# Seven-product weight pairs of a hybrid decoder trunk: the rounded weights times both activation parts in one matmul, and a weight sum made by DMA inside SBUF

## The chip, the cores and the metric

The kernel runs on one core of a Trainium2 chip. The metric is the device time of one execution in microseconds (us), the median of several runs. The engines are named as the profile names them: PE (TensorE matmuls), PEld (its weight loads), DVE (VectorE), ACT (ScalarE), POOL (GpSimd), SP (SyncE, which here only issues transfers).

## The reference

Two residual layers on x of 512 positions by 2048 features, all in float32, and a final RMSNorm.

```python
def reference(...):
    h = x
    hn = rmsnorm(h, norm_w[0]); h = h + hybrid_layer(hn, ...)      # DeltaNet heads and dilated attention
    hn = rmsnorm(h, norm_w[1]); h = h + shortconv_layer(hn, ...)
    return rmsnorm(h, final_norm_w)

def shortconv_layer(h, w_in, conv_w, w_out):                       # w_in 2048 x 12288, w_out 3072 x 2048
    gate_b, gate_c, u, z = jnp.split(h @ w_in, 4, axis=-1)
    y = gate_b * causal_depthwise_conv(gate_c * u, conv_w)
    return (y * jax.nn.silu(z)) @ w_out
```

The change touches `h @ w_in` of the second layer alone.

## The kernel before, in words

Every weight matrix is read from HBM in blocks, split into a rounded part `w_hi` and a rest `w_lo` (ACT rounds, DVE subtracts), and each product of float32 numbers is made of three matmuls in a fast format: hi by x_hi, hi by x_lo, lo by x_hi. Layer one and the last projection do so with 512 columns (`mm3`, L149 to L154).

`h @ w_in` of layer two is 96 blocks of 128 outputs. They are computed two at a time by `pair` (L867), 48 times, each as a 2 by 2 block product with seven half-size products instead of eight: weights `wa` and `wb` (two output blocks) are halved along the features, the activation is halved along features and positions, and seven sums or differences of the activation quarters (`forms`, made once, L771) are kept as tiles `fm`, each 128 by 256 in a rounded and a rest part. One product (`product`, L856) walks j over 8 blocks of 128 features and issues three matmuls of 256 columns per j (L862 to L864). So there are 48 x 7 x 8 = 2688 steps j.

The seven products of a pair, here P1 to P7, go into three PSUM banks: P1 and P5 into `acc`, P2, P4 and P6 into `sb`, P3 and P7 into `sc`. Their weights are in this order q11, q11 + s1, s3, s1, q12, q12 + (q11 + s1), q22. The raw tiles q11, s1, s3, q12 and q22 hold 512 KB each: five SP transfers from HBM (L870, L872, L873, L875, L876), and on POOL two transfers that add from HBM into SBUF (L871 into s1, L874 into s3). The two other sums are DVE additions (L884 for q11 + s1, L903 for q12). Raw tiles come from eight buffers, two of pool `wp` and `NRAW` = 6 of pool `w4`.

`split_w` (L849) takes the next of three `w_hi` and three `w_lo` buffers. So the split for one product can start only when the product three places earlier has used its buffer up: the split for P1 waits for P5 of the pair before, that for P2 for P6.

PE runs its instructions in the written order. The other engines' order is set by a list scheduler at build time, with loads and splits raised in priority by `SPLIT_AHEAD`; on the chip each engine then takes its own list strictly in order. Results are taken out of PSUM 256 columns at a time (ACT copies at L882 and L901, DVE at L888, L896, L897, L906, L910).

Of the kernel before, what the change touches and what calls it, by code (L numbers as in the profile page):

```python
# [14 lines left out]
P = 128  # L15
T = 512
# [14 lines left out]
NMT2 = 4 * NCH  # L31
NX2 = 24
NJ1 = 3
NRAW = 6
SPLIT_AHEAD = 600


# [37 lines left out]
def hybrid_trunk(ctx: ExitStack, tc: tile.TileContext, xT, w1, w1o, w2, w2o, nw, dcw, scw, hp, dnw, cst, msk, rope,  # L75
                 out, dbg=None):
    nc = tc.nc
    V, A, G, PE, SP = nc.vector, nc.scalar, nc.gpsimd, nc.tensor, nc.sync
    flow = Flow()
# [9 lines left out]
    def bank(name="m"):  # L89
        return mp.tile([P, T], F32, name=name, tag="m")  # L90
# [77 lines left out]
    def new_acc():  # L168
        return acc_p.tile([P, T], F32, name="acc")
# [34 lines left out]
    first = []  # L204
    with tc.tile_pool(name="ini", bufs=3) as ini:
# [29 lines left out]
        first = accs  # L235
# [334 lines left out]
    with tc.tile_pool(name="dn", bufs=2, side="right") as dn:  # L570
# [135 lines left out]
        for g in range(QKH):  # L706
# [52 lines left out]
    H = T // 2  # L759
    NJ = KT // 2  # L760
    rd2 = []
    slots = iter([(x2p, "x2", NX2)] * NX2 + [(xp, "x", 32)] * 32)
    fm = [[None] * NJ for _ in range(7)]

    def form(i, j, src):
        pool, tag, bufs = next(slots)
        t = pool.tile([P, 2, H], F32R, name="fm", tag=tag, bufs=bufs)
        A.activation(t[:, 0, :], src, AF.Copy)
        V.tensor_tensor(t[:, 1, :], src, t[:, 0, :].bitcast(F32), op=ALU.subtract)  # L769
        fm[i][j] = (t[:, 0, :], t[:, 1, :])  # L770

    def forms(pool, j, he, ho):
        e1, e2, o1, o2 = he[:, 0:H], he[:, H:T], ho[:, 0:H], ho[:, H:T]
# [65 lines left out]
    with tc.tile_pool(name="w4", bufs=1) as w4, tc.tile_pool(name="sc", bufs=1, side="right") as sc:  # L839

        def raw():
            i = nraw[0]
            nraw[0] += 1
            pool, tag, bufs = ((wp, "w_raw", 2), (w4, "w_raw4", NRAW))[i % (2 + NRAW) >= 2]
            return pool.tile([P, NJ, P], F32, name="w_raw", tag=tag, bufs=bufs)

        nraw = [0]

        def split_w(src):  # L849
            hi = wp.tile([P, NJ, P], F32R, name="w_hi", tag="w_hi", bufs=3)  # L850
            A.activation(hi, src, AF.Copy)  # L851
            lo = wp.tile([P, NJ, P], F32R, name="w_lo", tag="w_lo", bufs=3)
            V.tensor_sub(lo, src, hi.bitcast(F32))  # L853
            return hi, lo

        def product(w, f, o, first):  # L856
            hi, lo = w
            o = o[:, 0:H]
            for j in range(NJ):
                flow.poll()  # L860
                xh, xl = fm[f][j]
                PE.matmul(o, hi[:, j, :], xh, start=first and j == 0, stop=False, skip_group_check=not first)  # L862
                PE.matmul(o, hi[:, j, :], xl, start=False, stop=False, skip_group_check=not first)  # L863
                PE.matmul(o, lo[:, j, :], xh, start=False, stop=j == NJ - 1, skip_group_check=not first)  # L864
                flow.t += 0.36

        def pair(wa, wb, c1, c2):  # L867
            with tc.high_priority(offset=SPLIT_AHEAD):
                q11, s1, s3, q12, q22 = (raw() for _ in range(5))
                SP.dma_start(s1, wb[:, 0:NJ, :])  # L870
                G.dma_start(s1, wb[:, NJ:KT, :], accum_op=ALU.add)  # L871
                SP.dma_start(q11, wa[:, 0:NJ, :])  # L872
                SP.dma_start(s3, wa[:, 0:NJ, :])  # L873
                G.dma_start(s3, wb[:, 0:NJ, :], accum_op=ALU.add)  # L874
                SP.dma_start(q12, wa[:, NJ:KT, :])  # L875
                SP.dma_start(q22, wb[:, NJ:KT, :])  # L876
            a, b, c = new_acc(), bank("sb"), bank("sc")
            with tc.high_priority(offset=SPLIT_AHEAD):
                w = split_w(q11)
            product(w, 0, a, True)  # L880
            a1 = sc.tile([P, H], F32, name="a1", bufs=2)
            A.activation(a1, a[:, 0:H], AF.Copy)  # L882
            with tc.high_priority(offset=SPLIT_AHEAD):
                V.tensor_tensor(q11, q11, s1, op=ALU.add)  # L884
                w = split_w(q11)
            product(w, 5, b, True)
            e = sc.tile([P, H], F32, name="e", bufs=2)
            V.tensor_tensor(e, b[:, 0:H], a1, op=ALU.add)  # L888
            with tc.high_priority(offset=SPLIT_AHEAD):
                w = split_w(s3)  # L890
            product(w, 6, c, True)
            with tc.high_priority(offset=SPLIT_AHEAD):
                w = split_w(s1)
            product(w, 4, b, False)
            b2 = sc.tile([P, H], F32, name="b2", bufs=1)
            V.tensor_tensor(b2, b[:, 0:H], a1, op=ALU.add)  # L896
            V.tensor_tensor(c2[:, H:T], c[:, 0:H], b2, op=ALU.subtract)  # L897
            with tc.high_priority(offset=SPLIT_AHEAD):
                w = split_w(q12)
            product(w, 1, a, False)  # L900
            A.activation(c1[:, 0:H], a[:, 0:H], AF.Copy)  # L901
            with tc.high_priority(offset=SPLIT_AHEAD):
                V.tensor_tensor(q12, q12, q11, op=ALU.add)  # L903
                w = split_w(q12)
            product(w, 2, b, False)
            V.tensor_tensor(c1[:, H:T], b[:, 0:H], a1, op=ALU.add)  # L906
            with tc.high_priority(offset=SPLIT_AHEAD):
                w = split_w(q22)
            product(w, 3, c, False)
            V.tensor_tensor(c2[:, 0:H], c[:, 0:H], e, op=ALU.subtract)  # L910

        def ctile(w=T):
            return sc.tile([P, w], F32, name="ct", tag="ct", bufs=6)

        rbc2 = sc.tile([P, T], F32, name="rbc2")
        for c in range(NCH):
            cc, cu = ctile(), ctile(T + 2)
            G.memset(cu[:, 0:2], 0.0)
            u = cu[:, 2:T + 2]
            pair(w2[4 * c], w2[4 * c + 1], cc, u)  # L920
            if c == 0:
                flow.drain()
# [12 lines left out]
            V.scalar_tensor_tensor(gz, gz, 1.0, cz, op0=ALU.add, op1=ALU.mult)
            V.tensor_tensor(gz, gz, cc, op=ALU.mult)
            yt = sc.tile([P, T], F32, name="y2", bufs=2)
            V.scalar_tensor_tensor(yt, cb, 0.5, gz, op0=ALU.mult, op1=ALU.mult)
            if c < NCH - 1:
                SP.dma_start(Y2d[c], yt)  # L940
        ys = [None] * NCH
        for c in range(NCH):
            if c < NCH - 1:
                yl = sc.tile([P, T], F32, name="yl", tag="ct", bufs=6)
                SP.dma_start(yl, Y2d[c])
            else:
                yl = yt
            ys[c] = split_y(PX if c < 16 else (x2p, "x2", NX2), yl)
# [129 lines left out]
```

## Time and profile before

| | us |
|---|---|
| median of 3 runs (2819.26 to 2821.29) | 2820.0 |
| the profiled execution: its own time | 2821.6 |
| the profiled execution: span of the trace | 2819.8 |
| PE busy in the span | 2774.8 |
| DVE, ACT, POOL busy | 1798.9, 1091.6, 160.6 |
| the 48 pairs, by the first and last start of L862 | 1549.7 to 2526.2 |

The span is one profiled execution. Matmuls overlap in a pipeline, so a matmul's own duration is longer than the distance from one start to the next; the distance is what the stage costs. PEclk is the granted clock of TensorE as a share of 2.4 GHz, so 0.50 is 1.2 GHz. "To landing" of a transfer counts from its issue to its last byte. A name in square brackets behind a row is what ended the engine's idle time before it.

### The profile page before, as it was taken

How to read it: one execution, taken by the hardware profiler on the slowest of the kernel's cores; microseconds unless marked ns; L12 is line 12 of the kernel's file. 1: busy time of each engine (PE TensorE's matmuls, PEld its weight loads, DVE VectorE, ACT ScalarE, POOL GpSimd, SP SyncE). 2: the span in 40 equal slices, each digit the busy share in tenths (PEclk: the TensorE clock that was granted, in tenths of full speed). 3: DMA queues.
4: the chain of work that ended last, by engine and by line, in shares of the span. 5: the costliest groups of instructions: out<-in, count | busy, mean ns of one | idle time of the engine just before them, and what ended most of it. 6: DMA issues, size and time to landing. Idle time of an engine off the chain costs nothing.

```text
span 2819.8 us, 41852 instructions
## 1 busy us (share of the span) xinstructions
PE 2774.8 (98%) x16648; PEld 2463.6 (87%) x16648; DVE 1798.9 (64%) x2707; ACT 1091.6 (39%) x1803; POOL 160.6 (6%) x226
## 2 busy tenths in 40 slices
PE   8999999999999999999999899999999999999998
PEld 6888888888887888888887899999999999997887
DVE  7766999555445655665334677777777777774223
ACT  5443444444432323234323444444444444443221
POOL 3110000000000000000000100000000000000000
PEclk9999999999999999999999999999999999999999
DMA  5655223322224333333444767776677676754333
GB/s 170 183 169 186 90 87 127 111 88 86 94 86 127 124 105 110 115 113 112 127 127 135 217 181 200 186 204 182 190 191 197 187 191 188 194 164 141 114 112 112
DMA packets 163059, 410.58 MB, mean 146 GB/s; under 512 B 41184, under 2 KB 55776, under 8 KB 162608
## 3 DMA queue, kind: packets, MB, share of 16 engines
q1 hardware_dynamic: 149040, 357.57, 39.4%
q0 software_dynamic: 13824, 50.34, 10.1%
q8 instruction: 131, 2.15, 0.3%
q14 instruction: 64, 0.52, 0.1%
HBM read 373.44 MB, written 34.41 MB: 145 GB/s over the span
## 4 chain that ended last, share of the span: by engine, by line
PE 93%; DVE 3%; DMA 2%; issue 1%; ACT 1%; SPq 0%; DVEq 0%; POOL 0%; ACTq 0%; POOLq 0%
PE acc L151 17%; PE acc L153 17%; PE acc L152 17%; PE sb L862 5%; PE sb L864 5%; PE sb L863 5%; PE sc L862 3%; PE sc L864 3%; PE acc L862 3%; PE acc L864 3%; PE sc L863 3%; PE acc L863 3%; PE p L96 2%; DMA w_raw<-in_w_dram 1%; DVE w_lo L146 1%
## 5 line engine op out<-in xcount | busy, mean ns | idle before, releaser
L151 PE MATMUL acc<-x_hi,w_hi 128*128 128x512 f32 x1536 | 622.5, 405 | 1.6 <-DVE cv_raw L319 1.6
L153 PE MATMUL acc<-x_hi,w_lo 128*128 128x512 f32 x1536 | 602.3, 392 | 5.1 <-DVE w_lo L146 5.1
L152 PE MATMUL acc<-x_lo,w_hi 128*128 128x512 f32 x1536 | 600.6, 391 | 0.5 <-DVE x_lo L200 0.3
L144 ACT ACTIVATE w_hi<-w_raw 128x1024 fp32r<-128x1024 f32 (+2 forms) x302 | 308.9, 1024 | 683.9 <-PE acc L152 513.9
L851 ACT ACTIVATE w_hi<-w_raw 128x1024 fp32r<-128x1024 f32 x336 | 356.3, 1061 | 559.2 <-PE acc L863 165.8
L146 DVE TENSOR_TENSOR w_lo<-w_raw,w_hi 128x1024 fp32r<-128x1024 f32 (+2 forms) x302 | 363.6, 1206 | 315.1 <-ACT w_hi L144 314.4
L853 DVE TENSOR_TENSOR w_lo<-w_raw,w_hi 128x1024 fp32r<-128x1024 f32 x336 | 411.0, 1224 | 160.9 <-ACT w_hi L851 159.0
L153 PEld LDWEIGHTS acc<-x_hi,w_lo 128*128 128x128 f32 x1536 | 289.2, 188 | 69.6 <-DVE w_lo L146 7.2
L151 PEld LDWEIGHTS acc<-x_hi,w_hi 128*128 128x128 f32 x1536 | 290.1, 189 | 57.4 <-DVE cv_raw L319 1.8
L152 PEld LDWEIGHTS acc<-x_lo,w_hi 128*128 128x128 f32 x1536 | 290.3, 189 | 55.8 <-DVE x_lo L200 1.8
L862 PE MATMUL sb<-fm,w_hi 128*128 128x256 f32 x1152 | 325.9, 283 | 0.0
L864 PE MATMUL sb<-fm,w_lo 128*128 128x256 f32 x1152 | 325.2, 282 | 0.0
L863 PE MATMUL sb<-fm,w_hi 128*128 128x256 f32 x1152 | 324.5, 282 | 0.0
L151 PE MATMUL acc<-y_hi,w_hi 128*128 128x512 f32 (+1 forms) x792 | 307.6, 388 | 4.8 <-ACT y_hi L732 3.2
L152 PE MATMUL acc<-y_lo,w_hi 128*128 128x512 f32 (+1 forms) x792 | 305.7, 386 | 3.5 <-DVE y_lo L734 3.5
L153 PE MATMUL acc<-y_hi,w_lo 128*128 128x512 f32 (+1 forms) x792 | 305.8, 386 | 1.2 <-DVE w_lo L146 1.2
L862 PE MATMUL sc<-fm,w_hi 128*128 128x256 f32 x768 | 218.0, 284 | 5.5 <-ACT w_hi L851 5.5
L862 PEld LDWEIGHTS sb<-fm,w_hi 128*128 128x128 f32 x1152 | 219.7, 191 | 0.0
L863 PEld LDWEIGHTS sb<-fm,w_hi 128*128 128x128 f32 x1152 | 218.9, 190 | 0.0
L864 PEld LDWEIGHTS sb<-fm,w_lo 128*128 128x128 f32 x1152 | 218.5, 190 | 0.0
L864 PE MATMUL sc<-fm,w_lo 128*128 128x256 f32 x768 | 217.5, 283 | 0.5 <-DVE w_lo L853 0.5
L863 PE MATMUL acc<-fm,w_hi 128*128 128x256 f32 x768 | 216.0, 281 | 1.3 <-DVE fm L769 1.3
(241 smaller groups left out, 4322.5 us busy)
## 6 DMA issues: line engine op xcount, KB each, us to landing
w_raw<-in_w_dram SPq DMA_DIRECT2D x428, 512.0 KB, 4.4
w_raw<-in_w_dram POOLq DMA_DIRECT2D x96, 512.0 KB, 7.1
w_raw<-in_w1o_dram SPq DMA_DIRECT2D x48, 512.0 KB, 3.6
w_raw<-in_w2o_dram SPq DMA_DIRECT2D x48, 512.0 KB, 3.6
Y2d<-y SPq DMA_DIRECT2D x23, 256.0 KB, 5.3
yl<-Y2d SPq DMA_DIRECT2D x23, 256.0 KB, 4.4
xr<-in_xT_dram SPq DMA_DIRECT2D x16, 256.0 KB, 4.3
KQd<-kq SPq DMA_DIRECT2D x8, 512.0 KB, 5.1
```

The lines of the kernel that those rows point to most:

```text
L96: PE.matmul(o, lhsT, rhs, start=start, stop=stop)
L144: A.activation(hi, raw, AF.Copy)
L146: V.tensor_sub(lo, raw, hi.bitcast(F32))
L151: PE.matmul(acc, hi, xh, start=first, stop=False)
L152: PE.matmul(acc, hi, xl, start=False, stop=False)
L153: PE.matmul(acc, lo, xh, start=False, stop=last)
L851: A.activation(hi, src, AF.Copy)
L853: V.tensor_sub(lo, src, hi.bitcast(F32))
L862: PE.matmul(o, hi[:, j, :], xh, start=first and j == 0, stop=False, skip_group_check=not first)
L863: PE.matmul(o, hi[:, j, :], xl, start=False, stop=False, skip_group_check=not first)
L864: PE.matmul(o, lo[:, j, :], xh, start=False, stop=j == NJ - 1, skip_group_check=not first)
```

## The change

In `product`, a step j issues two matmuls: the rounded weights times both parts of `fm` side by side (512 columns, L861), and the rest of the weights times the rounded part (256 columns, L863). The left half of the bank then holds hi by x_hi plus lo by x_hi, the right half hi by x_lo. Copies and sums out of PSUM become 512 wide, and a new DVE addition `folded` (L868) adds the two halves, twice per pair. PE's list shrinks from 15691 to 13003 rows, which is by 2688.

In `pair`, q11 is split for P1 as soon as it is there; s3 is begun by an ACT copy of q11 (L877) instead of a second transfer from HBM; and q11 + s1 is made by a third POOL transfer, which adds s1 to q11 from SBUF to SBUF (L879), instead of a DVE addition. `NRAW` is 5.

```diff
-NRAW = 6
+NRAW = 5
...
-                PE.matmul(o, hi[:, j, :], xh, start=first and j == 0, stop=False, skip_group_check=not first)
-                PE.matmul(o, hi[:, j, :], xl, start=False, stop=False, skip_group_check=not first)
-                PE.matmul(o, lo[:, j, :], xh, start=False, stop=j == NJ - 1, skip_group_check=not first)
-                flow.t += 0.36
+                fx = fm[f][j]
+                PE.matmul(o, hi[:, j, :], fx.rearrange("p a t -> p (a t)"), start=first and j == 0, stop=False,
+                          skip_group_check=not first)
+                PE.matmul(o[:, 0:H], lo[:, j, :], fx[:, 0, :], start=False, stop=j == NJ - 1,
+                          skip_group_check=not first)
+                flow.t += 0.346
+
+        def folded(dst, w):
+            V.tensor_tensor(dst.rearrange("p (a t) -> p a t", a=2), w[:, :, 0:H], w[:, :, H:T], op=ALU.add)
...
                 SP.dma_start(s1, wb[:, 0:NJ, :])
                 G.dma_start(s1, wb[:, NJ:KT, :], accum_op=ALU.add)
                 SP.dma_start(q11, wa[:, 0:NJ, :])
-                SP.dma_start(s3, wa[:, 0:NJ, :])
+                w0 = split_w(q11)
+                A.activation(s3, q11, AF.Copy)
                 G.dma_start(s3, wb[:, 0:NJ, :], accum_op=ALU.add)
+                G.dma_start(q11, s1, accum_op=ALU.add)
                 SP.dma_start(q12, wa[:, NJ:KT, :])
                 SP.dma_start(q22, wb[:, NJ:KT, :])
...
-                w = split_w(q11)
-            product(w, 0, a, True)
-            a1 = sc.tile([P, H], F32, name="a1", bufs=2)
-            A.activation(a1, a[:, 0:H], AF.Copy)
-            with tc.high_priority(offset=SPLIT_AHEAD):
-                V.tensor_tensor(q11, q11, s1, op=ALU.add)
                 w = split_w(q11)
             product(w, 5, b, True)
-            e = sc.tile([P, H], F32, name="e", bufs=2)
-            V.tensor_tensor(e, b[:, 0:H], a1, op=ALU.add)
+            e = sc.tile([P, T], F32, name="e", bufs=1)
+            V.tensor_tensor(e, b, a1, op=ALU.add)
...
-            V.tensor_tensor(c2[:, H:T], c[:, 0:H], b2, op=ALU.subtract)
+            w2t = sc.tile([P, 2, T], F32, name="ww", tag="ww", bufs=2)
+            V.tensor_tensor(w2t[:, 1, :], c, b2, op=ALU.subtract)
...
-            V.tensor_tensor(c1[:, H:T], b[:, 0:H], a1, op=ALU.add)
+            V.tensor_tensor(w1t[:, 1, :], b, a1, op=ALU.add)
+            folded(c1, w1t)
...
-            V.tensor_tensor(c2[:, 0:H], c[:, 0:H], e, op=ALU.subtract)
+            V.tensor_tensor(w2t[:, 0, :], c, e, op=ALU.subtract)
+            folded(c2, w2t)
```

Two places show how the lists move. On POOL, about the middle of the stage, before (w_raw_17268 and w_raw_17502 are the s1 tiles of two pairs that follow each other, w_raw_17269 and w_raw_17503 their s3 tiles):

```order
L871 DMA w_raw_17268<-in_w2_dram 128x1024
L874 DMA w_raw_17269<-in_w2_dram 128x1024
L871 DMA w_raw_17502<-in_w2_dram 128x1024
L874 DMA w_raw_17503<-in_w2_dram 128x1024
L918 MEMSET ct_17499 128x2
L871 DMA w_raw_17733<-in_w2_dram 128x1024
L874 DMA w_raw_17734<-in_w2_dram 128x1024
```

and after (w_raw_17362, 17544 and 17723 are q11 of three pairs that follow each other; one, two and so on higher are s1 and s3 of the same pair):

```order
L874 DMA w_raw_17545<-in_w2_dram 128x1024
L879 DMA w_raw_17362<-w_raw_17363 128x1024
L924 MEMSET cu_17542 128x2
L878 DMA w_raw_17546<-in_w2_dram 128x1024
L874 DMA w_raw_17724<-in_w2_dram 128x1024
L879 DMA w_raw_17544<-w_raw_17545 128x1024
L878 DMA w_raw_17725<-in_w2_dram 128x1024
```

Each pair has a third transfer, L879, and in the pairs shown the s1 transfer of the pair that follows stands just ahead of it; over the whole list that is so in 27 of 48 pairs.

On DVE, before, from the last split of a pair (w_raw_17271, its q22) to the third of the next (w_raw_17501 is its q11, 17502 its s1, 17503 its s3):

```order
L853 TENSOR_TENSOR w_lo_17463<-w_raw_17271,w_hi_17461 128x1024
L853 TENSOR_TENSOR w_lo_17518<-w_raw_17501,w_hi_17516 128x1024
L884 TENSOR_TENSOR w_raw_17501<-w_raw_17501,w_raw_17502 128x1024
L906 TENSOR_TENSOR ct_17265<-sb_17280,a1_17310 128x256
L932 TENSOR_TENSOR ct_17265<-ct_17265,rbc_84 128x512
L853 TENSOR_TENSOR w_lo_17549<-w_raw_17501,w_hi_17547 128x1024
L910 TENSOR_TENSOR ct_17266<-sc_17281,e_17341 128x256
L935 SCALAR_TENSOR_TENSOR gzs_17491<-gzs_17491,ct_17265 128x512
L853 TENSOR_TENSOR w_lo_17579<-w_raw_17503,w_hi_17577 128x1024
```

and after, the same place (w_raw_17366 is the q22 of the pair that ends, w_raw_17544 the q11 of the next):

```order
L853 TENSOR_TENSOR w_lo_17513<-w_raw_17366,w_hi_17511 128x1024
L853 TENSOR_TENSOR w_lo_17554<-w_raw_17544,w_hi_17552 128x1024
L910 TENSOR_TENSOR ww_17486<-sb_17380,a1_17398 128x512
L868 TENSOR_TENSOR ct_17360<-ww_17486 128x512
L938 TENSOR_TENSOR ct_17360<-ct_17360,rbc_84 128x512
L915 TENSOR_TENSOR ww_17464<-sc_17381,e_17420 128x512
L941 SCALAR_TENSOR_TENSOR gzs_17534<-gzs_17534,ct_17360 128x512
L868 TENSOR_TENSOR ct_17361<-ww_17464 128x512
L942 TENSOR_TENSOR gzs_17534<-gzs_17534,ct_17180 128x512
L944 SCALAR_TENSOR_TENSOR y2_17538<-ct_17361,gzs_17534 128x512
L853 TENSOR_TENSOR w_lo_17584<-w_raw_17544,w_hi_17582 128x1024
L853 TENSOR_TENSOR w_lo_17606<-w_raw_17546,w_hi_17604 128x1024
```

The addition L884 between the first and the second split of q11 is gone from DVE, and the second split now stands behind the output work of the pair that ends.

## Rows read from the trace of the kernel before

**Rows 1.** The page: busy time of each engine, share of the span, instructions.

```profile
PE 2774.8 (98%) x16648; PEld 2463.6 (87%) x16648; DVE 1798.9 (64%) x2707; ACT 1091.6 (39%) x1803; POOL 160.6 (6%) x226
```

**Rows 2.** Busy time by stretch, 200 us inside the stage; first row: columns.

```profile
core 0: us, PE busy (x) PEld busy (x) DVE busy (x) ACT busy (x) POOL busy (x), PEclk, DMA share, GB/s
...
1800.00:2000.00 200.00, 200.00 (x1679) 200.00 (x1678) 155.03 (x185) 85.40 (x101) 18.66 (x26) 1.00 0.72 191
```

**Rows 3.** Timeline of PE, 256-column matmuls (start us, us, engine, line, names).

```profile
1600.00 0.29 PE L864 MATMUL sb<-fm,w_lo 128*128 128x256 f32 x1
...
1603.95 0.28 PE L864 MATMUL sc<-fm,w_lo 128*128 128x256 f32 x1
```

**Rows 4.** Timeline of PE: 512-column matmuls, then a 512 followed by a 256.

```profile
1001.04 0.39 PE L151 MATMUL acc<-x_hi,w_hi 128*128 128x512 f32 x1
...
1002.40 0.39 PE L151 MATMUL acc<-x_hi,w_hi 128*128 128x512 f32 x1
...
320.83 0.40 PE L153 MATMUL acc<-x_hi,w_lo 128*128 128x512 f32 x1
321.06 0.28 PE L484 MATMUL s_ps<-rh 128*128 128x256 f32 x1
```

**Rows 5.** Timeline, where a pair ends and the next one's splits begin.

```profile
1899.39 0.28 PE L862 MATMUL sb<-fm,w_hi 128*128 128x256 f32 x1
...
1899.52 1.06 ACT L851 ACTIVATE w_hi<-w_raw 128x1024 fp32r<-128x1024 f32 x1 [1.81 <-PE acc L863]
...
1900.62 1.23 DVE L853 TENSOR_TENSOR w_lo<-w_raw,w_hi 128x1024 fp32r<-128x1024 f32 x1 [1.31 <-ACT w_hi L851]
1901.88 1.22 DVE L884 TENSOR_TENSOR w_raw<-w_raw 128x1024 f32<-128x1024 f32 x1
...
1904.31 1.23 DVE L853 TENSOR_TENSOR w_lo<-w_raw,w_hi 128x1024 fp32r<-128x1024 f32 x1 [0.87 <-ACT w_hi L851]
...
1903.21 1.06 ACT L851 ACTIVATE w_hi<-w_raw 128x1024 fp32r<-128x1024 f32 x1 [2.36 <-DVE w_raw L884]
...
1907.99 0.28 PE L862 MATMUL sb<-fm,w_hi 128*128 128x256 f32 x1
```

**Rows 6.** Transfers that add: landing of L871, of L874; issue; queue share (1560 to 2520).

```profile
DMA to landing us min/median/max: 5.3/8.1/9.2
...
DMA to landing us min/median/max: 5.4/6.2/9.8
...
L871 POOL DMA_DIRECT2D w_raw<-in_w_dram x38 | 32.8, 863 | 408.8 <-DMA w_raw<-in_w_dram 317.0 <-DVE w_raw L903 31.8 <-DVE w_lo L853 23.6
...
q0 software_dynamic: 13674, 49.79, 29.3%
```

**Rows 7.** The page: plain transfers from HBM in the stage ahead (median us last).

```profile
w_raw<-in_w1o_dram SPq DMA_DIRECT2D x48, 512.0 KB, 3.6
```

**Rows 8.** Timeline of PE and stretches about idle times of PE (columns of rows 2).

```profile
1565.81 0.58 PE L862 MATMUL sc<-fm,w_hi 128*128 128x256 f32 x1 [5.47 <-ACT w_hi L851]
...
1565.80:1567.00 1.20, 0.80 (x2) 0.50 (x2) 1.20 (x2) 1.20 (x2) 0.05 (x1) 0.50 1.06 224
...
1572.00:1574.00 2.00, 2.00 (x19) 2.00 (x19) 0.69 (x1) 1.51 (x2) 0.83 (x1) 1.00 0.95 377
...
1554.58 0.39 PE L863 MATMUL acc<-fm,w_hi 128*128 128x256 f32 x1 [1.25 <-DVE fm L769]
...
1558.45 0.28 PE L864 MATMUL sb<-fm,w_lo 128*128 128x256 f32 x1
...
1556.00:1558.00 2.00, 2.00 (x11) 2.00 (x11) 0.87 (x3) 0.00 (x0) 0.00 (x0) 0.50 0.92 223
...
2529.00:2532.00 3.00, 1.33 (x4) 0.59 (x4) 2.35 (x5) 0.95 (x3) 0.00 (x0) 1.00 0.84 283
```

**Rows 9.** Groups by line, 1640 to 2400 us: a 256-wide and a 512-wide addition.

```profile
L906 DVE TENSOR_TENSOR ct<-sb,a 128x256 f32<-128x256 f32 x38 | 15.9, 418 | 0.0
L932 DVE TENSOR_TENSOR ct<-ct,rbc 128x512 f32<-128x512 f32 x19 | 13.2, 693 | 2.0
```

More of the change, by code (lines that the diff above doesn't have):

```diff
@@ L769, in form @@
         V.tensor_tensor(t[:, 1, :], src, t[:, 0, :].bitcast(F32), op=ALU.subtract)
-        fm[i][j] = (t[:, 0, :], t[:, 1, :])
+        fm[i][j] = t
     def forms(pool, j, he, ho):
@@ L857, in product @@
             hi, lo = w
-            o = o[:, 0:H]
             for j in range(NJ):
                 flow.poll()
-                xh, xl = fm[f][j]
-                PE.matmul(o, hi[:, j, :], xh, start=first and j == 0, stop=False, skip_group_check=not first)
-                PE.matmul(o, hi[:, j, :], xl, start=False, stop=False, skip_group_check=not first)
-                PE.matmul(o, lo[:, j, :], xh, start=False, stop=j == NJ - 1, skip_group_check=not first)
-                flow.t += 0.36
+                fx = fm[f][j]
[6 more added lines that the diff above has]
+            V.tensor_tensor(dst.rearrange("p (a t) -> p a t", a=2), w[:, :, 0:H], w[:, :, H:T], op=ALU.add)
         def pair(wa, wb, c1, c2):
@@ L877, in pair @@
             a, b, c = new_acc(), bank("sb"), bank("sc")
+            product(w0, 0, a, True)
+            a1 = sc.tile([P, T], F32, name="a1", bufs=2)
+            A.activation(a1, a, AF.Copy)
             with tc.high_priority(offset=SPLIT_AHEAD):
                 w = split_w(q11)
-            product(w, 0, a, True)
-            a1 = sc.tile([P, H], F32, name="a1", bufs=2)
-            A.activation(a1, a[:, 0:H], AF.Copy)
-            with tc.high_priority(offset=SPLIT_AHEAD):
-                V.tensor_tensor(q11, q11, s1, op=ALU.add)
-                w = split_w(q11)
             product(w, 5, b, True)
-            e = sc.tile([P, H], F32, name="e", bufs=2)
-            V.tensor_tensor(e, b[:, 0:H], a1, op=ALU.add)
+            e = sc.tile([P, T], F32, name="e", bufs=1)
+            V.tensor_tensor(e, b, a1, op=ALU.add)
             with tc.high_priority(offset=SPLIT_AHEAD):
@@ L894, in pair @@
             product(w, 4, b, False)
-            b2 = sc.tile([P, H], F32, name="b2", bufs=1)
-            V.tensor_tensor(b2, b[:, 0:H], a1, op=ALU.add)
-            V.tensor_tensor(c2[:, H:T], c[:, 0:H], b2, op=ALU.subtract)
+            b2 = sc.tile([P, T], F32, name="b2", bufs=1)
+            V.tensor_tensor(b2, b, a1, op=ALU.add)
+            w2t = sc.tile([P, 2, T], F32, name="ww", tag="ww", bufs=2)
+            V.tensor_tensor(w2t[:, 1, :], c, b2, op=ALU.subtract)
             with tc.high_priority(offset=SPLIT_AHEAD):
@@ L900, in pair @@
             product(w, 1, a, False)
-            A.activation(c1[:, 0:H], a[:, 0:H], AF.Copy)
+            w1t = sc.tile([P, 2, T], F32, name="ww", tag="ww", bufs=2)
+            A.activation(w1t[:, 0, :], a, AF.Copy)
             with tc.high_priority(offset=SPLIT_AHEAD):
@@ L909, in pair, with ctile @@
             product(w, 3, c, False)
-            V.tensor_tensor(c2[:, 0:H], c[:, 0:H], e, op=ALU.subtract)
-        def ctile(w=T):
-            return sc.tile([P, w], F32, name="ct", tag="ct", bufs=6)
+            V.tensor_tensor(w2t[:, 0, :], c, e, op=ALU.subtract)
+            folded(c2, w2t)
+        def ctile():
+            return sc.tile([P, T], F32, name="ct", tag="ct", bufs=4)
         rbc2 = sc.tile([P, T], F32, name="rbc2")
         for c in range(NCH):
-            cc, cu = ctile(), ctile(T + 2)
+            cc, cu = ctile(), sc.tile([P, T + 2], F32, name="cu")
             G.memset(cu[:, 0:2], 0.0)
@@ L936, in hybrid_trunk @@
             V.tensor_tensor(gz, gz, cc, op=ALU.mult)
-            yt = sc.tile([P, T], F32, name="y2", bufs=2)
+            yt = sc.tile([P, T], F32, name="y2", bufs=1)
             V.scalar_tensor_tensor(yt, cb, 0.5, gz, op0=ALU.mult, op1=ALU.mult)
@@ L943, in hybrid_trunk @@
             if c < NCH - 1:
-                yl = sc.tile([P, T], F32, name="yl", tag="ct", bufs=6)
+                yl = sc.tile([P, T], F32, name="yl", tag="ct", bufs=4)
                 SP.dma_start(yl, Y2d[c])
```

## The prediction

> **What bounds the kernel now.** I read the page's busy times first, then the stretches of time inside the 48 pairs, then single matmuls, then one pair's border on all engines.
>
> PE is busy for 98% of the span [rows 1], and inside the pairs for all of it, at the full clock of 2.4 GHz, while DVE has 155 of 200 us and ACT 85 [rows 2]. So in this stage the time is the number of matmuls times the distance of their starts. At 256 columns there are 33 starts in 3.95 us, 0.1197 us each [rows 3]; at 512 columns six in 1.36 us, 0.2267 us each [rows 4]. Those are 13.0 and 13.4 ns more than the columns take at 2.4 GHz (106.7 and 213.3 ns): a matmul has a fixed price of 13 ns. A step j now takes 3 x 0.1197 = 0.359 us, a product of eight steps 2.87 us, a pair 20.1 us. A 512 followed by a 256 keeps the 512's distance, 0.23 us [rows 4].
>
> Second, the border of two pairs [rows 5]. Call T0 the start of P6, 1899.39: P5 has just used up the split buffers that the next pair's P1 wants. ACT rounds for P1 0.13 us later, DVE starts the rest 1.10 us after that, and both for P2 follow: DVE adds s1 to q11 (1901.88), ACT rounds at 1903.21, DVE's rest is ready at 1905.5. P2's first matmul comes at 1907.99, which is T0 + 8.60, three products after T0. There are some 2.5 us of slack, and the addition stands inside that chain.
>
> **The change, part by part.**
>
> *Matmuls.* A step becomes 0.2267 + 0.1197 = 0.3464 us, 12.7 ns less; 2688 steps give 34 us, 0.71 us per pair. A product then takes 2.77 us, and P2 would begin at T0 + 8.31. The rows say that the fixed price is 13 ns. The Trainium skill ("TensorE: Matmul & The Clock Gate", section "Back-to-back issue gap") has the distance of warm matmuls as the columns' time plus 2.5 ns; by that the fusion would save only 2688 x 2.5 ns = 7 us. The rows speak against it here, and I take 34.
>
> *The sum q11 + s1 by DMA.* This is the term that decides. The addition takes 1.22 us on DVE now [rows 5]; it becomes a POOL transfer between the first and the second split of the same tile. It can't begin before DVE has made P1's rest (it overwrites what DVE reads), and P2's rounding can't begin before it has landed. P1's split can't go earlier, since it waits for P5's buffers. The chain, by [rows 5]: rounding at T0 + 0.13, rest from T0 + 1.23 to T0 + 2.46, issue at T0 + 2.5. In 27 of 48 pairs the next pair's s1 transfer stands just ahead on POOL's list; one issue is 0.86 us [rows 6], so 0.48 us on average: T0 + 3.0. Then the landing. No row shows a transfer from SBUF to SBUF that adds. The nearest are L871 and L874, which add from HBM, of the same size: medians 8.1 and 6.2 us, from 5.3 to 9.8 [rows 6]. I take 6.2, the value of the line with less beside it, since here nothing comes from HBM and a pair will have one load less. That is T0 + 9.2; ACT's rounding and DVE's rest take another 2.4 (1903.21 to 1905.54): T0 + 11.6. P2's first matmul with `w_lo` would have come at T0 + 8.31 + 0.23 = T0 + 8.54. **PE stands still for 3.0 us in every pair** (1.7 with a landing of 5.3 and nothing ahead, 7.0 with 9.8 and a whole issue ahead). Nothing gives it back, as PE has no other idle time in the stage and the next pair's chain again starts from its own P5.
>
> Behind the waiting rounding stand on ACT the roundings for P3 and P4 and the copy of P1's result, on DVE the rests for P3 and P4. They catch up while P2 runs: P3's rest is there some 1.9 us after P2's (one 512-wide operation of the output work, 0.69 us, and one rest, 1.23 us), and P2 lasts 2.77.
>
> *The clock.* After 5.47 us of idleness PE came back at a granted clock of 0.50, which is 1.2 GHz, from 1565.8 to 1572; 6.2 us at half speed lose 3.1 us. After a shorter idle time of 1.25 us the half clock lasted at most from 1554.6 to 1558.4, so it lost up to 1.9 us [rows 8]. There is one stretch that speaks against it: from 2529 to 2532 PE was busy for only 1.33 of 3 us and the clock stayed at 1.00 [rows 8]. Here PE would be nearly without work for 3 us once per pair, with one matmul inside it. I take a loss of 2.2 us per pair, nearer to the short case; the ends are 0 and 3.1.
>
> *The rest.* Five results per pair become 512 wide, 0.69 instead of 0.42 us on DVE [rows 9], two foldings of 0.69 are added and an addition of 1.22 is gone: +1.5 us of DVE per pair, 15.6 to 17.1 of 20. It lies beside PE's work (88% of a pair of 19.4 us, less of a longer one); if PE did not cover it, 1.5 x 48 = 72 us. On ACT the copy of q11 into s3 (as long as a rounding, 1.06 us [rows 5]) and two wider copies (taken as DVE's 0.27 each [rows 9]) make 1.6 us on 8.6 [rows 2], covered likewise; the copy stands in the order ahead of the chain and waits for q11's load alone. The transfer of s3 from HBM that goes away was hidden, so it gives nothing; SP issues four weight loads per pair instead of five. Seven raw buffers instead of eight let loads start later. The splits of [rows 5] wait for PE, ACT or DVE and none for a load, so I set it to 0; a load fully exposed would be 3.6 us per pair [rows 7].
>
> *Sum.* Per pair 3.0 + 2.2 - 0.7 = 4.5 us, 216 us over 48 pairs. The profiled execution took 2821.6, 1.6 over the median of the runs: 2821.6 + 216 - 1.6 = **3036 us**.
>
> **The rivals.**
>
> *The sum lands late, the clock holds.* For it: the stretch at 2529 us. Then (3.0 - 0.7) x 48 = 110, 2930 us; with the shortest landing, 5.3, and the same average wait on POOL (2.1 - 0.7) x 48 = 67, 2887 us.
>
> *The s1 transfer ahead holds the engines too.* The 94 adding transfers took 29.3% of the 16 DMA engines in 960 us [rows 6], 3.0 us each with all engines. If the sum waits for the whole transfer ahead in 27 of 48 pairs, that is 1.7 us more on average: 6.2 us per pair, 298 us, 3118. For it: L871's landings reach 9.2 with a least of 5.3. Against it: the order puts both close together only in those pairs.
>
> *The sum lands in time: faster.* Everything hangs on one number. With a landing under 8.54 - 2.4 - 3.0 = 3.1 us (3.6 where nothing stands ahead on POOL) P2's rest is ready when PE comes to it, no idle time arises, the clock stays up, and what is left is the matmuls' gain: 2820 - 34 = 2786 us. For it: plain loads from HBM land in 3.6 us in a calm stage [rows 7], and a sum inside SBUF reads nothing from HBM. Against it: all 96 adding transfers took 5.3 us or more. The Trainium skill ("DMA: Bandwidth & Descriptors", section "Anatomy of one DMA, SWDGE (gpsimd) path") gives a transfer issued by GpSimd 2.0 us and its bytes at 436 KB per us; for 512 KB I work out an estimate of 3.2 us, which would all but hide it. The adding transfers of this trace are at twice that.
>
> *The change does less than it says on PE.* If the 512s cost more than in layer one, 0.7 us per pair are lost, 34 us on top of any case. A 512 next to a 256 has been seen at its price [rows 4], so this has no chance of its own.
>
> **How the numbers follow.** The forecast 0.58; late with the clock held 0.15; with the transfer ahead 0.17; in time 0.08; 0.02 for something between that cancels out. The range must leave out the in-time case and can leave out the shortest landings with a held clock and the longest landings: from 2900 to 3190 us (7.7 us per pair, a landing of 9.4). A difference of 0.2%, 6 us, is about what a measurement of this kernel can tell. Faster 0.08, same 0.02, slower 0.90.
>
> **What would show it.** Right: idle time of PE ahead of L861 in `sb`, once per pair and about 2 to 5 us long; ACT's L851 waiting for the transfer L879, whose landing is 5 to 9 us; PEclk at half for some us behind each; between the stops 0.227 and 0.120 us per matmul. Wrong on the main step: L879 landing within 3.6 us, or L851 for P1 starting before P5 has ended. Wrong on the clock: PEclk at 1.00 through the stage. If instead PE waits for DVE with L879 long landed, the 17 us of DVE per pair were the limit; if it waits for SP's loads, the seventh buffer was.

## The result and the profile after

The changed kernel takes 3104.8 us (3095.7 to 3109.6, six runs), against 2820.1 us of the kernel before on the same chip: 1.1008 times as long, 95% interval 1.0989 to 1.1027, 285 us slower. The forecast was 3036 us, with a range from 2900 to 3190.

The page of the changed kernel answers to [rows 1]: PE falls from 98% to 92% of a span that is 278 us longer, and the granted clock is below full speed in every few slices of the second half.

```profile
PE 2856.2 (92%) x13960; PEld 2381.8 (77%) x13960; DVE 1870.1 (60%) x2755; ACT 1148.5 (37%) x1851; POOL 203.1 (7%) x274
...
PEclk9999999999999999999989898989889898998999
...
L861 PE MATMUL sb<-fm,w_hi 128*128 128x512 f32 x1152 | 485.4, 451 | 165.9 <-ACT w_hi L851 165.9
...
L863 PE MATMUL sb<-fm,w_lo 128*128 128x256 f32 x1152 | 362.1, 314 | 29.3 <-DVE w_lo L853 29.3
```

The two groups of `sb` matmuls now have 195 us of idle time of PE ahead of them (last column, with what ended it), all of it at P2: first for the rounding of its weights on ACT, then for the rest on DVE. Before there was none ahead of `sb` matmuls. For the third transfer, L879, the trace shows what ACT waited for, and how long the transfer takes:

```profile
L879 POOL DMA_DIRECT2D w_raw<-w_raw x48: 864/868/1237, 1551.5 to 2770.1; - x48
...
  ACT w_hi L851: 303.5, 44
...
DMA to landing us min/median/max: 4.6/7.3/12.0
```

ACT waited 303.5 us for it, in 44 of 48 pairs; the landing is 7.3 us in the median. This is the border of two pairs as in [rows 5], now of the changed kernel, merged from the timelines of SP, PE, ACT, POOL and DVE (P6 of the pair ahead began at 1916.4; the number in front is the start, then the length in us):

```profile
1915.62 0.33 SPq L873 DMA_DIRECT2D w_raw<-in_w_dram  x1
...
1916.50 1.06 ACT L851 ACTIVATE w_hi<-w_raw 128x1024 fp32r<-128x1024 f32 x1 [1.74 <-PE acc L861]
...
1917.59 1.23 DVE L853 TENSOR_TENSOR w_lo<-w_raw,w_hi 128x1024 fp32r<-128x1024 f32 x1 [0.27 <-ACT w_hi L851]
...
1919.30 0.86 POOL L874 DMA_DIRECT2D w_raw<-in_w_dram  x1 [8.18 <-DVE w_lo L853]
1919.89 1.16 POOL L879 DMA_DIRECT2D w_raw<-w_raw  x1
...
1924.60 0.28 PE L863 MATMUL acc<-fm,w_lo 128*128 128x256 f32 x1
...
1927.72 2.95 ACT L851 ACTIVATE w_hi<-w_raw 128x1024 fp32r<-128x1024 f32 x3 [5.50 <-DMA w_raw<-w_raw]
...
1928.83 0.53 PE L861 MATMUL sb<-fm,w_hi 128*128 128x512 f32 x1 [3.95 <-ACT w_hi L851]
1930.09 0.58 PE L863 MATMUL sb<-fm,w_lo 128*128 128x256 f32 x1 [0.74 <-DVE w_lo L853]
```

It reads downwards: the next pair's load of s1 from HBM (it lands at 1918.74), rounding and rest for P1, the transfer that adds to that s1, the sum's transfer right behind it, the end of P1 on PE, 7.8 us after the sum's issue the rounding for P2, then PE. The clock falls here: from P2's first matmul with `w_lo` on it is 0.50.

```profile
1929.36:1931.50 2.14, 1.41 (x4) 1.26 (x5) 2.14 (x3) 1.79 (x3) 0.00 (x0) 0.50 0.00 0
```

POOL's list also shows why the neighbour costs more than its own issue. The s1 transfer must wait for the load that it adds to: in all 27 borders where it stands ahead, it goes out 0.5 to 0.8 us after that load has landed (the profile names that load in 16 of the 27; here it names DVE's `w_lo`, which ended within 0.1 us of the landing), and the sum behind it waits with it.

And this is a border where nothing stood ahead on POOL (P6 began at 1787.6): issue at 1790.36, ACT's rounding 4.7 us later, P2's first matmul 0.2 us late.

```profile
1790.36 0.86 POOL L879 DMA_DIRECT2D w_raw<-w_raw  x1 [7.93 <-DVE w_lo L853]
1792.23 0.86 POOL L874 DMA_DIRECT2D w_raw<-in_w_dram  x1 [1.01 <-DMA w_raw<-in_w_dram]
...
1795.02 2.95 ACT L851 ACTIVATE w_hi<-w_raw 128x1024 fp32r<-128x1024 f32 x3 [5.73 <-DMA w_raw<-w_raw]
...
1796.13 0.50 PE L861 MATMUL sb<-fm,w_hi 128*128 128x512 f32 x1
1797.39 0.39 PE L863 MATMUL sb<-fm,w_lo 128*128 128x256 f32 x1 [0.76 <-DVE w_lo L853]
```

**Where the 278 us of span went.** I took from PE's timeline the first matmul of every pair. From the second pair to the last, 46 distances, a pair takes 25.71 us instead of 20.05: 260 us. The first pair, while the stage starts, takes 6.6 us more. And from the stage's last matmul to the end of the span's last matmul there are 294.0 us instead of 283.0, mostly since the last projection waits longer for its activations (14.9 us instead of 6.7): 11.0 us.

Within a pair, call lateness the time by which P2's first matmul with `w_lo` comes after T0 + 8.54, and the rest of a pair's distance over 19.40 us plus its lateness the loss. Over these 46 pairs the lateness is 4.55 us and the loss 1.76 us. It can be laid out by what stands ahead of L879 on POOL (47 borders):

| border | count | issue of L879 after T0 | from issue to ACT's rounding | lateness |
|---|---|---|---|---|
| the next pair's s1 transfer less than 4 us ahead | 27 | 4.24 us | 8.04 us | 6.10 us |
| not so | 20 | 2.85 us | 5.61 us | 2.30 us |

The loss goes by the lateness: of the ten pairs late by less than 2.2 us nine lose 0.15 to 0.24 us, and all 36 pairs late by more lose 1.26 to 2.92. The granted clock accounts for it: in 37 of the 46 pairs it is 0.50 for a while, in the nine it stays at 1.00, and the time at 0.50 from P2's first matmul with `w_lo` on, at half speed, comes to 1.74 us per pair, against the loss of 1.76. In single stretches: the pair above, late by 1.25 us, keeps 1.00 through its wait (1795.9 to 1798.0); the next one, late by 2.29, does not. The columns are those of [rows 2].

```profile
1795.90:1798.00 2.10, 1.33 (x7) 0.76 (x6) 1.89 (x3) 2.10 (x4) 0.00 (x0) 1.00 0.85 166
...
1817.00:1819.00 2.00, 0.50 (x1) 0.19 (x1) 1.04 (x1) 2.00 (x3) 0.00 (x0) 1.00 1.01 197
1819.00:1821.00 2.00, 1.76 (x8) 1.52 (x9) 2.00 (x4) 1.30 (x2) 0.00 (x0) 0.74 0.28 87
1821.00:1823.00 2.00, 2.00 (x8) 1.71 (x8) 1.06 (x1) 0.00 (x0) 0.00 (x0) 0.50 0.69 177
1823.00:1825.00 2.00, 2.00 (x12) 1.72 (x11) 1.06 (x2) 1.06 (x1) 0.00 (x0) 0.91 0.91 313
```

### The profile page after: what moved, and what is told of

The parts are those of the page before. It is cut to its first block, busy times and chain, and to the rows that moved or that the text cites. A ratio compares the mean times of both kernels' runs of the same rounds, so it can differ in the third digit from the quotient of the medians.

```text
span 3097.6 us, 36686 instructions
## 1 busy us (share of the span) xinstructions
PE 2856.2 (92%) x13960; PEld 2381.8 (77%) x13960; DVE 1870.1 (60%) x2755; ACT 1148.5 (37%) x1851; POOL 203.1 (7%) x274
## 4 chain that ended last, share of the span: by engine, by line
PE 71%; DMA 16%; DVE 7%; ACT 4%; issue 2%; POOL 0%; SPq 0%; ACTq 0%; POOLq 0%; DVEq 0%
PE acc L151 16%; PE acc L153 16%; PE acc L152 16%; DMA w_raw<-w_raw 10%; PE sb L861 7%; PE sb L863 4%; DVE w_lo L853 4%; DMA w_raw<-in_w_dram 4%; ACT w_hi L851 3%; PE sc L861 2%; PE p L96 2%; PE acc L861 2%; PE sc L863 1%; PE acc L863 1%; DMA yl<-Y2d 1%
## 5 line engine op out<-in xcount | busy, mean ns | idle before, releaser
L861 PE MATMUL sb<-fm,w_hi 128*128 128x512 f32 x1152 | 485.4, 451 | 165.9 <-ACT w_hi L851 165.9
L851 ACT ACTIVATE w_hi<-w_raw 128x1024 fp32r<-128x1024 f32 x336 | 345.0, 1054 | 640.4 <-DMA w_raw<-w_raw 303.5
L861 PEld LDWEIGHTS sb<-fm,w_hi 128*128 128x128 f32 x1152 | 251.9, 219 | 238.4 <-ACT w_hi L851 181.4
L863 PE MATMUL sb<-fm,w_lo 128*128 128x256 f32 x1152 | 362.1, 314 | 29.3 <-DVE w_lo L853 29.3
L863 PEld LDWEIGHTS sb<-fm,w_lo 128*128 128x128 f32 x1152 | 252.1, 219 | 49.1 <-DVE w_lo L853 49.1
L861 PE MATMUL sc<-fm,w_hi 128*128 128x512 f32 x768 | 276.2, 399 | 0.0
L861 PE MATMUL acc<-fm,w_hi 128*128 128x512 f32 x768 | 272.2, 394 | 2.5 <-DVE fm L769 2.5
L863 PE MATMUL sc<-fm,w_lo 128*128 128x256 f32 x768 | 215.5, 281 | 0.0
L863 PE MATMUL acc<-fm,w_lo 128*128 128x256 f32 x768 | 214.1, 279 | 0.0
L151 PEld LDWEIGHTS acc<-y_hi,w_hi 128*128 128x128 f32 x792 | 149.8, 189 | 47.0 <-ACT y_hi L732 16.7
```

Source lines behind the costliest of these rows:

```text
L151: PE.matmul(acc, hi, xh, start=first, stop=False)
L861: PE.matmul(o, hi[:, j, :], fx.rearrange("p a t -> p (a t)"), start=first and j == 0, stop=False, skip_group_check=not first)
L863: PE.matmul(o[:, 0:H], lo[:, j, :], fx[:, 0, :], start=False, stop=j == NJ - 1, skip_group_check=not first)
```

## The experiments

The theory is the forecast's: the sum's transfer stands between the two splits of q11, and P2 waits for it. The rivals: the wider results or the missing raw buffer cost the time; the landing is long because of the source, or of other transfers; what is lost behind the wait is not the clock.

**The sum by DVE again.** All of the change stays but the third transfer.

```diff
-                G.dma_start(q11, s1, accum_op=ALU.add)
...
             with tc.high_priority(offset=SPLIT_AHEAD):
+                V.tensor_tensor(q11, q11, s1, op=ALU.add)
                 w = split_w(q11)
             product(w, 5, b, True)
```

> The changed kernel with the sum q11 + s1 made by a DVE addition between the two splits, as before the change; everything else of the change stays (512-column matmuls, foldings, s3 begun by the ACT copy, seven raw buffers). Theory (the landing of the third transfer inside the split chain is the whole loss): PE's idle time ahead of P2 goes, the clock stays up, and the time is that before less the matmuls' gain, 2820 - 34 = 2786 us, within 15. Rival (the wider results and foldings load DVE too much, or seven buffers are too few): DVE has some 18.3 us per pair of 19.4, P2 or another product still comes late, and the time is 2830 us or more.

Measured: 2796.8 us (2795.8 to 2797.8), 0.9924 of the kernel before, interval 0.9907 to 0.9940. The lateness is 0.06 us in every pair, the loss 0.05, a pair takes 19.51 us. In the stretch inside the stage PE is busy throughout at full clock, and DVE for 731 of 800 us:

```profile
1640.00:2440.00 800.00, 800.00 (x4595) 699.22 (x4594) 730.70 (x840) 407.29 (x451) 72.95 (x102) 1.00 0.66 169
```

So one line of the change holds all of the loss, and the rest of it is a gain. It is 11 us over the expected 2786. Five are 46 pairs of 19.51 instead of 19.40. Another part is the hand-over to the last projection: from the end of the stage's last matmul to the end of the span's last there are 291.7 us, before 283.0.

**The matmul part alone**, with s3 loaded from HBM as before and still seven raw buffers.

```diff
-                w0 = split_w(q11)
-                A.activation(s3, q11, AF.Copy)
+                SP.dma_start(s3, wa[:, 0:NJ, :])
...
-                G.dma_start(q11, s1, accum_op=ALU.add)
...
-            product(w0, 0, a, True)
+            with tc.high_priority(offset=SPLIT_AHEAD):
+                w = split_w(q11)
+            product(w, 0, a, True)
...
+                V.tensor_tensor(q11, q11, s1, op=ALU.add)
...
```

> The matmul part alone: 512-column matmuls and foldings, with the loads and sums of the kernel before (s3 from HBM, q11 + s1 on DVE), still seven raw buffers. Theory: 2786 us as in the run with the DVE addition, since ACT's copy and the load of s3 are both hidden; within 8 us of that run. Rival (the ACT copy that begins s3, or the load of s3, costs something): the two runs differ by over 10 us.

Measured: 2824.2 us (2816.3 to 2826.2), 1.0017, interval 1.0008 to 1.0027. The rival is right: 27 us more than with the ACT copy. ACT now waits for loads, 58.5 us in 14 pieces (9.2 us in two with the copy), DMA is busy for 0.73 of the stage instead of 0.66, and from 1640 to 2440 us PE starts 4487 matmuls instead of 4595:

```profile
  DMA w_raw<-in_w_dram: 58.5, 14
```

With seven raw buffers the fifth load of a pair from HBM takes the gain of the matmuls away; the ACT copy, which the prediction booked as giving nothing, makes up for the missing buffer. That it is the buffers is argued from these waits: PE itself waits in this stretch for DVE (7.8 us for `e`, 3.0 for a rest) and not for a load by name, and the matmul part with eight buffers was not run.

**The DMA part alone**, on the matmuls before, with eight raw buffers.

```diff
-                SP.dma_start(s3, wa[:, 0:NJ, :])
+                w0 = split_w(q11)
+                A.activation(s3, q11, AF.Copy)
                 G.dma_start(s3, wb[:, 0:NJ, :], accum_op=ALU.add)
+                G.dma_start(q11, s1, accum_op=ALU.add)
...
-                V.tensor_tensor(q11, q11, s1, op=ALU.add)
...
```

> The kernel before with the DMA part alone: q11 split first, s3 begun by the ACT copy, q11 + s1 by the third POOL transfer; three 256-column matmuls per step and eight raw buffers as before. Theory (the transfer is the whole loss, the matmul part a gain): P2 is wanted 0.3 us later than with the fused matmuls, the s1 transfer stands ahead in 46 pairs, lateness 5 to 6 us and a half clock of 1.9 us per pair: 2819 + 48 x 7 = 3155 us, from 3110 to 3230. Rival (part of the loss belongs to the 512-column matmuls and wider results): clearly under 3105 us.

Measured: 3165.7 us (3161.4 to 3172.3), 1.1238, interval 1.1219 to 1.1257. It is slower than the full change, as the theory has it: the DMA part costs 347 us here, and the fused matmuls only reduce its bill. A pair takes 27.30 us instead of 20.05. The next pair's s1 transfer is issued ahead of the sum's in 46 pairs, as expected, and in 35 of them the next pair's s3 transfer stands between the two as well. L876 is the transfer's line in this kernel:

```profile
  ACT w_hi L851: 362.5, 47
...
DMA to landing us min/median/max: 4.5/7.5/13.1
```

**POOL's order.** The 48 pairs run with POOL's list in the written order, so the next s1 transfer stands behind the sum's.

```diff
+        pool_order = tc.manual_schedule(engines={mybir.EngineType.PE, mybir.EngineType.Pool})
+        pool_order.__enter__()
         for c in range(NCH):
...
+        pool_order.__exit__(None, None, None)
```

> The changed kernel with POOL's list kept in the written order through the 48 pairs, so that the sum q11 + s1 stands ahead of the next pair's s1 transfer in all pairs (it stands behind it in 27 of 48 in the changed kernel, and those pairs were 6.1 us late, the other 20 looked at 2.3). Theory (the s1 transfer just ahead costs issue time and landing): all pairs are late by 2.3 to 3.4 us, median landing of L879 under 6.5 us, some pairs keep the clock; 2797 + 48 x (2.8 + 1.2) = 2990 us, from 2950 to 3040. Rival (the long landings come from other traffic at that time of the pair): the time stays within 30 us of 3105.

Measured: 3053.6 us (3048.3 to 3056.0), 1.0830, interval 1.0814 to 1.0846. Between the two: 51 us faster than the changed kernel, not 115. The median landing falls from 7.3 to 6.6 us and the mean lateness to 3.77. But the pairs now alternate: those with no s1 transfer within 8 us of L879 are late by 1.2 to 3.9 us, the others by 3.4 to 6.7, and of these 23 L879 is issued at T0 + 3.6 or later in 16, while in the other seven the pair's own s1 transfer went out only 7 us ahead of it. In the 16 the sum waits for its own source: it is issued 0.5 us (once 0.8) after the pair's s1 transfer, held back by the new order, has landed. The order moved a part of the wait and did not remove it.

**The source of the transfer.**

```diff
-                G.dma_start(q11, s1, accum_op=ALU.add)
+                G.dma_start(q11, wb[:, 0:NJ, :], accum_op=ALU.add)
```

> The changed kernel with the third transfer reading 512 KB of wb from HBM instead of s1 from SBUF (it leaves out the right sum q11 + s1: q11 + the first half of wb stands in its place). Theory (the landing is set by what shares POOL's rings and the 16 engines, not by the source): L879 lands as before, median 7.3 us with a least of 4.6, and the time is within 25 us of 3105. Rival (a source in SBUF is slower or faster): median landing differs by 1 us or more, 48 us or more in time.

Measured in a single run: 3139.3 us, 34 over the changed kernel; L879 lands at

```profile
DMA to landing us min/median/max: 5.3/8.0/12.3
```

The source in SBUF is 0.7 us quicker at the least and in the median. A pair takes 26.67 us instead of 25.71: 0.81 us more lateness, 0.15 more loss. The time falls between what the theory and the rival had (within 25 us, 48 or more). So the source counts a little, less than what stands ahead (8.04 against 5.61 us in the table above; the s1 transfer is ahead in 27 borders here too). The landing of a transfer that adds is long from either.

**The clock.** Sixteen matmuls into a PSUM bank that nobody reads, between P1 and P2.

```diff
+            fill = bank("fill")
+            for _ in range(16):
+                PE.matmul(fill, w0[0][:, NJ - 1, :], fm[0][NJ - 1].rearrange("p a t -> p (a t)"), start=True, stop=True)
             product(w, 5, b, True)
```

> The changed kernel with 16 more 512-column matmuls (3.6 us) between P1 and P2, into a PSUM bank that nobody reads, while PE would be waiting. Theory (a pair that waits 2.3 us or more then runs at half clock for a while and loses 1.7 to 2.9 us): pairs late by up to some 5.5 us keep the clock and lose 0.2 us; pairs late by less than 3.9 us pay up to 2.6 us for the extra work; per pair about 0.5 us less in all, 3080 us, from 3040 to 3110, and the mean granted clock rises from 0.952. Rival (the loss behind the wait is not the clock but late splits): the loss per pair stays, the time rises by 20 us or more.

Measured: 3110.7 us (3105.6 to 3121.1), 1.1040, interval 1.1017 to 1.1062; no gain in time. But the mechanism shows. The mean clock of the execution rises from 0.952 to 0.982, and of the pairs late by 4 to 6.7 us, eleven lose 0.15 to 0.55 us, where in the changed kernel all such pairs lost 1.5 us or more. The mean loss falls from 1.76 to 1.01 us; of that the time at half clock is 0.61, where it was 1.74, and the remaining 0.4 us were not traced. The lateness rises from 4.55 to 5.39 us, since no pair can now be less than 3.7 us late, and in this build the s1 transfer stands ahead in 32 pairs. What the clock gave back the extra work and this remainder took, so the expected 3080 us were missed. Stretches of 800 us of the changed kernel and of this one:

```profile
1840.00:2640.00 800.00, 671.71 (x3426) 567.30 (x3425) 520.19 (x598) 301.67 (x339) 80.64 (x107) 0.89 0.61 146
```

```profile
1840.00:2640.00 800.00, 745.07 (x3932) 630.46 (x3930) 524.47 (x600) 298.94 (x339) 82.53 (x109) 0.97 0.60 147
```

**P2 moved back.** P3 before P2 covers 2.77 us of the chain, P3 and P5 before it 5.5.

```diff
             with tc.high_priority(offset=SPLIT_AHEAD):
+                w = split_w(s3)
+            product(w, 6, c, True)
+            with tc.high_priority(offset=SPLIT_AHEAD):
                 w = split_w(q11)
             product(w, 5, b, True)
...
-            with tc.high_priority(offset=SPLIT_AHEAD):
-                w = split_w(s3)
-            product(w, 6, c, True)
...
```

This is the first of the two; the second also moves P5, with the copy of its result, ahead of P2.

> The changed kernel with P2 and P3 exchanged (P1, P3, P2, P4 and so on): the weights that the transfer makes are wanted one product, 2.77 us, later. Theory (lateness is fixed by the chain from P1's split to the landing): each pair's lateness shrinks by 2.77 us, from 4.5 to about 2 on average (6.1 to 3.3 in the pairs with the next s1 transfer ahead, 0 to 0.5 in the others), the half clock stays in the first kind only; 2786 + 48 x 3.2 = 2940 us, from 2910 to 2970. Rival (POOL, the rings or DVE are loaded so that the transfer moves back with its user): lateness stays at 4 us or more, 3070 us or more.

> The changed kernel in the order P1, P3, P5, P2, P4, P6, P7: the transfer's sum is wanted two products, 5.5 us, later. Theory: a pair is late only where the chain took over 5.5 us too long, 0.5 to 1 us per pair on average, with half the clock loss; 2786 + 48 x 1.2 = 2844 us, from 2795 to 2880. Rival (moving it back moves the transfer too): 3000 us or more.

Measured: 3064.9 us (3055.7 to 3072.8), 1.0873 (1.0846 to 1.0899), and 2967.3 us (2964.2 to 2970.5), 1.0528 (1.0512 to 1.0543). Both are slower than the theory and faster than the rival had them, with a new wait in place of the old one. The waits of PE in the first of the two, from 1600 to 2700 us (us in total, times, longest):

```profile
PE sb L861 <- DVE e L893: 121.3, 45, 3.9
PE sb L863 <- DVE w_lo L853: 15.1, 22, 0.8
PE sb L861 <- ACT w_hi L851: 13.8, 14, 2.0
```

P2's own wait is nearly gone (13.8 and 15.1 us), but P4 follows P2 in the same bank and must wait until DVE has read P2's result. So both were run with a bank of their own for P4 and P6:

```diff
-            a, b, c = new_acc(), bank("sb"), bank("sc")
+            a, b, c, d = new_acc(), bank("sb"), bank("sc"), bank("sd")
...
-            product(w, 4, b, False)
+            product(w, 4, d, True)
...
-            V.tensor_tensor(b2, b, a1, op=ALU.add)
+            V.tensor_tensor(b2, d, e, op=ALU.add)
...
-            product(w, 2, b, False)
-            V.tensor_tensor(w1t[:, 1, :], b, a1, op=ALU.add)
+            product(w, 2, d, False)
+            V.tensor_tensor(w1t[:, 1, :], d, e, op=ALU.add)
...
```

> The order P1, P3, P2, P4 again, now with P4 and P6 in a PSUM bank of their own, so that P4 need not wait until DVE has read P2's result (121 us of waits in the run without the bank). Theory (lateness is the chain to the landing, and 2.77 us of it are now covered): lateness 1.5 to 2 us per pair, clock kept in over half of the pairs; 2797 + 48 x 2.5 = 2917 us, from 2880 to 2970. Rival (DVE's and ACT's lists push the transfer back): 3000 us or more.

> The order P1, P3, P5, P2, P4, P6, P7 with the bank of their own for P4 and P6. Theory: 5.5 us of the chain are covered, under 1 us of lateness per pair and little half clock; 2797 + 48 x 1 = 2845 us, from 2790 to 2890. If the transfer is fully covered it comes to the 2797 of the run with the DVE addition or some us below, as DVE has 1.2 us less to do. Rival (the transfer or its users on DVE move back): 2920 us or more.

Measured: 2975.4 us (2968.1 to 2981.3), 1.0551 (1.0532 to 1.0570), 5 us above the range that was expected, and 2968.3 us (2964.6 to 2971.9), 1.0531 (1.0513 to 1.0549), where the rival is right and the bank has changed nothing. The latter's waits and a piece of ACT's timeline:

```profile
PE acc L861 <- ACT a L885: 73.2, 32, 5.0
PE sd L861 <- DVE b L903: 42.0, 48, 0.9
```

```profile
1820.28 1.06 ACT L851 ACTIVATE w_hi<-w_raw 128x1024 fp32r<-128x1024 f32 x1 [3.12 <-DMA w_raw<-w_raw]
1821.24 0.58 ACT L885 ACTIVATE a<-acc 128x512 f32<-128x512 f32 x1
```

ACT takes its list in order. The rounding that waits for the transfer (3.12 us here) stands directly ahead of the copy of P1's result (L885), in 43 of 48 pairs, and P5, which has come forward, adds to the bank that this copy has to read first. So the products that were to cover the transfer wait behind it by way of ACT. An order of ACT that avoids this was not tried.

**The hand-over, and one more buffer.** On the run with the DVE addition, tiles of tag `ct` were added; they hold outputs and later the activations read back. In the one run they go from 4 to 6 and `NRAW` from 5 to 4, in the other from 4 to 5 and `a1` from two buffers to one.

> The run with the DVE addition (2797 us) with six instead of four tiles for the outputs and the activations read back (tag ct, as before the change), paid for by six instead of seven raw weight buffers. That run waited 13.5 us at the end of the stage for activations (before the change: 6.7). Theory (four such tiles are late reading back at the hand-over): these waits fall to 7 us, the time to 2790. Rival (raw buffers are what the stage lives on): splits wait for loads, and the time is over 2810 us.

> The run with the DVE addition with five such tiles, paid for by one instead of two tiles for P1's result. Theory: the waits at the hand-over fall by some 3 us, to 2793 us. Rival (the next pair's copy of P1's result waits for its only tile, and with it ACT's splits): a new wait of 0.2 to 1 us per pair, 2805 to 2840 us.

Measured: 2858.4 us (2852.2 to 2865.9), 1.0140 (1.0115 to 1.0164), and 2793.5 us (2791.2 to 2794.3), 0.9909 (0.9894 to 0.9924). The first shows both sides. Its waits at the hand-over fall from 13.5 to 8.0 us, and with six raw buffers ACT's roundings wait 89 us for loads and its copies into s3 another 51, where the run with seven had no such wait in the same stretch, 1600 to 2450 us:

```profile
ACT w_hi L851 <- DMA w_raw<-in_w_dram: 89.2, 26, 4.9
...
ACT w_raw L877 <- DMA w_raw<-in_w_dram: 50.9, 20, 4.6
```

The second is by its median the fastest kernel of this study, 26.5 us under the one before (3 us under the run with four tiles): fused matmuls, foldings, the ACT copy, the sum on DVE, five tiles. Its waits at the hand-over are 11.2 us:

```profile
PE acc L151 <- ACT y_hi L732: 9.9, 3, 7.1
PE acc L152 <- DVE y_lo L734: 1.3, 3, 0.8
```

## Why the prediction was right, and which terms were mis-sized

- **What bounds the kernel, and the chain.** Right. P1's split starts 0.1 us after P5 has used its buffers, the sum's transfer follows P1's rest, P2's rounding follows the landing. P1's last matmul starts 8.24 us after T0 in nearly every pair, so P2 could begin at some T0 + 8.36 where the forecast had 8.31. The run with the DVE addition shows that this one line of the change makes the kernel slower.
- **Matmuls, 0.71 us per pair.** Right, with a small rest: a pair without waits takes 19.51 us instead of 20.05, 0.54. Over 46 pairs that is 25 us, nearer to the 34 that came from the rows than to the 7. The gap that gave the 7 is stated by the Trainium skill ("TensorE: Matmul & The Clock Gate", "Back-to-back issue gap") for an isolated matmul, which the prediction left out. The trace does not agree with it for these matmuls, each with a weight load: 0.1197 us at 256 columns, 0.2267 at 512.
- **The standstill, 3.0 us per pair.** The mis-sized term: it measured 4.5. The forecast put the issue at T0 + 3.0 and the landing at 6.2; measured were T0 + 3.65 and 7.0 on average over 47 borders, 0.65 + 0.8 us too little. It took the median of L874, where traffic is thin, while the order already showed the s1 transfer right ahead in 27 of 48 pairs. Those 27 are late by 6.10 us, the others by 2.30, so the neighbour costs 3.8 us where it stands, 2.2 us on the mean. 2.4 of the 3.8 are a longer landing, which is the rival that the forecast priced at 3.0 us where the neighbour stands, 1.7 on the mean. The other 1.4 are a later issue: the forecast had 0.86 for the neighbour's issue and nothing for the load from HBM that the neighbour, and the sum behind it, wait for. Where nothing stood ahead, the forecast's landing was too long (5.6 us).
- **The clock, 2.2 us per pair.** Right in kind, a little high: 1.76, so that it made up for a part of what the standstill lacked. The case with the clock held was right for nine of 46 pairs, all late by 2.2 us or less.
- **The rest, booked at nothing.** In the run with the DVE addition the wider results and foldings cost no wait of PE that shows, with DVE busy for 91% of the stage. Seven raw buffers instead of eight cost nothing there either; by the run without the ACT copy, that is because the copy spares a load, which the prediction did not see. Whether an eighth buffer would bring the load that holds the sum back earlier in the changed kernel was not run. Not booked at all were the tiles of tag `ct` (6 to 4) and `y2` (2 to 1). The first bear on the waits at the hand-over: two tiles more take 5.5 us of them away, one more 2.3. The share of `y2` is not shown.
- **The rival that ends faster** needed a landing under 3.6 us. None was: the shortest of 48 took 4.6. From the fit that the Trainium skill ("DMA: Bandwidth & Descriptors", "Anatomy of one DMA, SWDGE (gpsimd) path") states for a transfer issued by GpSimd, the estimate is 3.2 us for 512 KB; the trace does not agree for transfers that add, whose median is 7.3 us here.

By the measured terms: (4.55 + 1.76 + 19.40 - 20.05) x 46 = 260 us, and with 6.6 us of the first pair and 11.0 of the hand-over 278 us, the difference of the spans. The first pair and the hand-over, together 18 us, were not in the forecast.

## What to carry to other kernels

Before an operation of 1.2 us on a half-idle engine becomes a transfer, look at what has to wait for it: a transfer that overwrites a tile between two uses of it puts its whole latency into the chain, here 7 us in a place with 2.5 us of slack. Read from the built order what stands ahead of it in its queue, since the neighbour decided more than the source did, and what the neighbour itself waits for. And moving the consumer back covers such a wait only in part while engines that take their lists in order hold other work behind it: here 2967 us at best, against 2797 without the transfer.

## What the runs showed of the hardware that was not expected

- A transfer of 512 KB that adds inside SBUF lands in 4.6 to 12.0 us, median 7.3; the same from HBM in 5.3 to 12.3, median 8.0 (one run). The source is worth 0.7 us; with another adding transfer less than 4 us ahead in POOL's queue the time to the rounding is 2.4 us longer (8.04 against 5.61), besides the later issue of 1.4 us.
- PE's clock falls and returns by pair: waits that made P2 late by up to 2.2 us left it at 1.00, 2.4 GHz, in nine of ten pairs, and all longer ones were followed by a stretch at 0.50, 1.2 GHz, that cost a further 1.3 to 2.9 us. Work that nobody reads kept it up in eleven pairs late by 4 to 6.7 us and gained nothing in time.
